# Scores of a head pair as half-row matmuls from shared tiles, and the norm's Newton turns on GpSimd

## The chip, the cores and the metric

The kernel runs on one core of a Trainium2 chip. The metric is the device time of one execution in microseconds, the median of several runs. TensorE (PE) multiplies, VectorE (DVE), ScalarE (ACT) and GpSimd (POOL) do the elementwise work, and DMAs are issued from SyncE's queue (SP).

## The reference

Two decoder layers over 1024 tokens of width 1024: a Mamba-2 layer, then a stick-breaking attention layer over 16 heads of 64 columns. Only the attention matters here. Key and query heads are RMS-normed over their 64 columns; the scores are the product over those 64 columns; the weights come from a running product along the keys.

```
k = rmsnorm(kv[..., :SB_WIDTH].reshape(bsz, s, SB_HEADS, SB_HEAD_DIM), k_g)
q = rmsnorm(qg[..., :SB_WIDTH].reshape(bsz, s, SB_HEADS, SB_HEAD_DIM), q_g)
...
z = jnp.einsum('bhtd,bhsd->bhts', q[:, :, q0:kend], k[:, :, :kend]).astype(jnp.float32)
log_keep = jnp.where(strict, jax.nn.log_sigmoid(-z), 0.0)
suffix = lax.cumsum(log_keep, axis=3, reverse=True) - log_keep
weights = jnp.where(strict, jnp.exp(jax.nn.log_sigmoid(z) + suffix), 0.0)
outs.append(jnp.einsum('bhts,bhsd->bhtd', weights.astype(v.dtype), v[:, :, :kend]))
```

## The kernel before

Every large product is made from two-part operands: a float is split into a high part (fp32r) and a low part (the rest), and three products are summed (high by high, high by low, low by high).

The attention (`attention`, from L860) goes over 8 head pairs `hp`; each pair has four steps, `p` = 3, 2, 1, 0, of 256 queries, so there are 32 steps `i`. A step projects queries, keys and values for its two blocks of 128 tokens (`project`, L923, 48 matmuls of 384 columns on L911), and at p = 1 the gate of the pair. `norm` (L1010) squares on ACT, sums on DVE (L1022), starts a reciprocal root on DVE (L1028 to L1030), improves it in three Newton turns of three small DVE instructions (L1034 to L1036, tiles of 128x8) and multiplies (`nmul`, L1043). `flip` (L1046) transposes keys and queries on PE (L1054) and splits them. In the kernel before each head has key tiles of its own in `kst`: the high part of head h in its own 64 partitions, the low part in the other 64 (L1064 on ACT, L1067 on DVE); `qh` holds the query's high part twice (L1076, four ACT copies a step), and `ql` holds the low part with zeros in the other half (L1081). So one matmul over all 128 rows gives high by high and high by low together (L1111), and a second one gives low by high (L1112).

`scores` (L1098) does that for one head h and one block of 128 queries b, in one piece up to 512 key columns or two pieces above that; then a sigmoid on ACT (L1119) and a scan on DVE (L1124). `combine` (L1130) transposes the scanned weights (L1150, L1152), splits them (L1158 ACT, L1163 DVE), and multiplies by the value differences (L1171). The value differences are formed on POOL (`values`: L997, L1006, L1007).

The order of the work is made by a planner (`Plan`, from L70): each operation is given with its engine, a cost in us, a rank, what it follows and which ring slots it takes or frees. `order()` always takes the operation that can start first by these costs, the smaller rank among equals (`RANK`, L44). The whole list is then issued in that order. For PE, ACT and DVE the list order is kept as it is (L1377); POOL and SP are not in that list, so their order is left to the framework. The score tiles `z` are a ring of two PSUM banks, the probability tiles `pt` a ring of five, `qh` of one.

Of the kernel before, what the change touches and what calls it, by code (L numbers as in the profile page):

```python
# [8 lines left out]
F32 = mybir.dt.float32  # L9
F32R = mybir.dt.float32r  # L10
# [3 lines left out]
ALU = mybir.AluOpType  # L14
# [4 lines left out]
P = 128  # L19
# [21 lines left out]
FILL = {32: 7, 33: 6}  # L41
CHUNKS = {29: (0, 1), 30: (2, 3)}

RANK = {"project": 3, "copy_kq": -13, "sums": -16, "start": -28, "newton": -2587, "nmul": -6, "v_split": -57,  # L44
        "gate": 20, "sig": 55, "gmul": -17, "w_load": 6, "w_hi": -28, "w_lo": -45, "k_hi": 10, "k_lo": -32,
        "q_hi": -853, "q_lo": -3, "scores": -1586, "s_sig": -729, "scan": 8, "turn": -2674, "a_hi": 20,
        "a_lo": 1, "o_add": -18, "o_gate": 27, "store": -4, "r_lo": -919, "o_load": 7, "o_hi": 6, "f_load": 13,
        "f_split": -10, "fill": -19, "f_add": -1544}


def split3(nc, out, pairs):
# [18 lines left out]
class Plan:  # L70
# [789 lines left out]
def attention(k, A, rawp, hT, oTd, dbg, b2, pairs):  # L860
# [6 lines left out]
    with ExitStack() as ctx:  # L867
# [13 lines left out]
        ql = pp.tile([P, 2, 256], F32R, name="ql")  # L881
        nc.gpsimd.memset(ql.bitcast(F32), 0.0)

        oqs = op.tile([P, 512], F32, name="oq")

        plan = Plan()
        for name, bufs in (("mm", 2), ("z", 2), ("tr", 3), ("w", 3), ("pt", 5), ("kq", 2), ("vr", 3), ("qh", 1), ("sg", 1),
                           ("of", 2), ("V", 6), ("vs", 1), ("raw", 3)):
            plan.ring(name, bufs)
        op_, slot = plan.op, plan.slot  # L890
# [119 lines left out]
        def norm(i, hp, p, copies):  # L1010
            g = {}
            sg_s = slot("sg")

            def square():
                g["sq"] = wk.tile([P, 512], F32, name="sg", bufs=1)
                nc.scalar.activation(g["sq"], sts[hp]["kq", p].rearrange("p b m c -> p (b m c)"), AF.Square)
            sq = op_("square", "ACT", 0.63, 10 * i + 1, square, copies, (sg_s,))
            m = 8

            def sums():  # L1020
                g["ss"] = sm.tile([P, m], F32, name="kss")
                nc.vector.reduce_sum(g["ss"], g["sq"].rearrange("p (g d) -> p g d", d=64), axis=AX.X)  # L1022
            rd = op_("sums", "DVE", 0.68, 10 * i + 1, sums, [sq], (), (sg_s,))

            def start():
                v, y = g["v"], g["y"] = [sm.tile([P, m], F32, name=x) for x in ("krv", "kry")]
                g["s"] = sm.tile([P, m], F32, name="krs")
                nc.vector.tensor_scalar(v, g["ss"], 1.0 / 64, EPS, op0=ALU.mult, op1=ALU.add)  # L1028
                nc.vector.tensor_single_scalar(y.bitcast(I32), v.bitcast(I32), 1, op=ALU.logical_shift_right)
                nc.vector.tensor_scalar(y.bitcast(I32), y.bitcast(I32), -1.0, float(0x5F3759DF), op0=ALU.mult, op1=ALU.add)  # L1030

            def turn_():
                v, y, s = g["v"], g["y"], g["s"]
# [12 lines left out]
        def flip(i, hp, p):  # L1046
# [10 lines left out]
            ks, qs = slot("tr", 2), slot("tr", 2)  # L1057
# [3 lines left out]
            qh_s = slot("qh", 2 * sum(len(parts(b)) for b in (2 * p + 1, 2 * p)))  # L1061

            def key_hi(h):
                return lambda: nc.scalar.activation(kst[own[h], h, tsl], t[0][own[h]], AF.Copy, scale=g[own[h]])  # L1064

            def key_lo(h):
                return lambda: nc.vector.scalar_tensor_tensor(  # L1067
                    kst[own[1 - h], h, tsl], t[0][own[h]], g[own[h]], kst[own[h], h, tsl].bitcast(F32),
                    op0=ALU.mult, op1=ALU.subtract)

            def query_hi(h):
                def go():
                    if h == 0:
                        tiles["qh", i] = wk.tile([P, 2, 256], F32R, name="qh", bufs=1)
                    for x in (own[h], own[1 - h]):
                        nc.scalar.copy(tiles["qh", i][x, h], t[1][own[h]])  # L1076
                return go

            def query_lo(h):
                o = own[h]  # L1080
                return lambda: nc.vector.tensor_tensor(ql[o, h], t[1][o], tiles["qh", i][o, h].bitcast(F32), op=ALU.subtract)  # L1081
            prev, pd = [], []
            for h in range(2):
                prev = [op_("k_hi", "ACT", 0.47, 10 * i + 2, key_hi(h), [fk] + prev + (old if p == 3 else []))]
                khi[i, h] = prev[0]
                pd = [op_("k_lo", "DVE", 0.49, 10 * i + 2, key_lo(h), [khi[i, h]] + pd, (), (ks,))]
                klo[i, h] = pd[0]
            for h in range(2):
                prev = [op_("q_hi", "ACT", 0.73, 10 * i + 2, query_hi(h), [fq] + prev, (qh_s,) if h == 0 else ())]
                pd = [op_("q_lo", "DVE", 0.43, 10 * i + 2, query_lo(h), prev + pd + old, (), (qs,))]  # L1090
                qlo[i, h] = pd[0]
# [6 lines left out]
        def scores(i, hp, h, b, qh_s):  # L1098
            N = (NT - b) * P
            qs = slice((b % 2) * P, (b % 2) * P + P)  # L1100
            pt_s[i, h, b] = slot("pt")
            key = ("a", hp, h, b)
            last = []
            sg = []
            for m, (ko, w) in enumerate(parts(b)):
                z_s = slot("z")

                def mul(ko=ko, w=w, m=m):
                    z = tiles["z", i, h, b, m] = zp.tile([P, 512], F32, name="z")
# [6 lines left out]
                def sig(ko=ko, w=w, m=m):  # L1116
                    if m == 0:
                        tiles[key] = wk.tile([P, S], F32, name="pt", bufs=5)
                    nc.scalar.activation(tiles[key][:, ko:ko + w], tiles["z", i, h, b, m][:, :w], AF.Sigmoid, scale=-1.0)  # L1119
                s = op_("s_sig", "ACT", 0.19 + w * 0.00078, 10 * i + 3, sig, [z] + sg, (pt_s[i, h, b],) if m == 0 else (), (z_s,))  # L1120

                def scan(ko=ko, w=w):
                    pt = tiles[key]
                    nc.vector.tensor_tensor_scan(pt[:, ko:ko + w], pt[:, ko:ko + w], keep[:, ko:ko + w],  # L1124
                                                 pt[:, ko - 1:ko] if ko else 1.0, op0=ALU.mult, op1=ALU.max)
                sg = [s]
                last = [z, op_("scan", "DVE", 0.15 + w * 0.00208, 10 * i + 3, scan, [s] + last[1:])]
            scans[i, h, b] = last[1]

        def combine(i, hp, p):  # L1130
            lo = 2 * p
# [207 lines left out]
        for hp in range(8):  # L1339
# [14 lines left out]
                begun.append(op_("begin", "SPW", 0.0, 0, lambda: b2.begin(pairs), proj[6, 0][-1:]))  # L1354
            for i, p in pair:
                qh_s = flip(i, hp, p)
                for h in range(2):
                    for b in (2 * p + 1, 2 * p):
                        scores(i, hp, h, b, qh_s)
                combine(i, hp, p)  # L1360
        for kk in range(KT):
            s_out(kk)
# [247 lines left out]
```

## Time and profile before

| what | value |
|---|---|
| median of 3 runs | 1757.9 us (1756.42 to 1758.44) |
| profiled execution | 1758.81 us |
| its span, first to last instruction | 1757.1 us |
| mean granted TensorE clock | 0.994 of full speed |
| PE busy | 1703.1 us (97%) |
| DVE busy | 1196.1 us (68%) |
| ACT busy | 895.9 us (51%) |
| POOL busy | 434.2 us (25%) |

The attention fills the stretch from about 930 to 1570 us; before it lies the Mamba layer and the first embedding, behind it the output projection and the second embedding. Instructions of PE are pipelined, so the shown duration of a matmul is longer than its share of the engine; the distance from the start of one to the start of the next is what it costs.

### The profile page before, as it was taken

The numbers are of one execution on the slowest core, as the hardware profiler recorded it, in microseconds if no ns is written. First come the engines' busy times: TensorE is split into PE (matmuls) and PEld (weight loads), VectorE is DVE, ScalarE is ACT, GpSimd is POOL, SyncE is SP. The second block draws the span as 40 slices with busy tenths as digits, with TensorE's granted clock in tenths as the row PEclk, the third lists the DMA queues.
The fourth block names the chain that finished last, engine by engine and source line by source line (L and its number), as shares of the span: only waits on it lengthen the run. The fifth ranks groups of instructions, "written<-read, shape, count | busy, mean of one in ns | idle before, by whom it ended". The sixth has DMA issues, their size and how long they took to land.

```text
span 1757.1 us, 25573 instructions
## 1 busy us (share of the span) xinstructions
PE 1703.1 (97%) x9170; PEld 1450.7 (83%) x9170; DVE 1196.1 (68%) x2460; ACT 895.9 (51%) x1976; POOL 434.2 (25%) x452
## 2 busy tenths in 40 slices
PE   7999999999999999999999999999999999899999
PEld 6777877887887777888888999989999998778887
DVE  7678179259448846443567699999999999993232
ACT  6558339447635624222355556666575666652121
POOL 0134624524444322220001111121121214211010
PEclk9999999999999999999999999999999999899999
DMA  4222213213212365332221111111110112252100
GB/s 162 69 67 91 96 49 108 90 54 96 91 66 79 126 215 179 113 132 87 82 100 31 56 32 59 41 33 56 31 59 28 48 43 67 76 165 78 57 28 36
DMA packets 96399, 139.43 MB, mean 79 GB/s; under 512 B 18160, under 2 KB 66640, under 8 KB 96272
## 3 DMA queue, kind: packets, MB, share of 16 engines
q1 hardware_dynamic: 96272, 137.80, 24.4%
q8 instruction: 72, 1.18, 0.3%
q14 instruction: 55, 0.45, 0.1%
HBM read 108.77 MB, written 24.77 MB: 76 GB/s over the span
## 4 chain that ended last, share of the span: by engine, by line
PE 79%; DVE 13%; ACT 4%; DMA 2%; issue 2%; POOL 0%; SPq 0%; DVEq 0%; ACTq 0%
PE mm L54 38%; PE mm L911 17%; PE mm L1441 4%; PE oq L1171 3%; DVE pt L1124 3%; PE pq L54 3%; DVE v L310 2%; PE intra L485 2%; PE z L1111 2%; PE z L1112 2%; PE tr L1150 1%; PE tr L740 1%; DVE wl L1163 1%; PE inter L480 1%; PE tr L1152 1%
## 5 line engine op out<-in xcount | busy, mean ns | idle before, releaser
L54 PE MATMUL mm<-ul,wh 128*128 128x512 f32 (+1 forms) x648 | 254.0, 392 | 0.0
L54 PE MATMUL mm<-uh,wh 128*128 128x512 f32 (+1 forms) x648 | 252.4, 390 | 0.1
L54 PE MATMUL mm<-uh,wl 128*128 128x512 f32 (+1 forms) x648 | 252.4, 390 | 0.0
L1124 DVE TENSOR_TENSOR_SCAN pt<-pt,keep 128x320 f32<-128x320 f32 (+3 forms) x192 | 196.1, 1048 | 3.5 <-ACT pt L1119 1.4
L911 PE MATMUL mm<-g0h,hh 128*128 128x384 f32 x512 | 174.7, 341 | 3.6 <-ACT vr L952 1.8
L911 PE MATMUL mm<-g0l,hh 128*128 128x384 f32 x512 | 175.9, 343 | 0.0
L911 PE MATMUL mm<-g0h,hl 128*128 128x384 f32 x512 | 174.2, 340 | 0.0
L310 DVE SCALAR_TENSOR_TENSOR v<-u,convh,v 128x512 f32<-128x512 f32 x144 | 129.5, 904 | 55.1 <-ACT v L308 52.6
L997 POOL TENSOR_TENSOR vs<-vs,vr 128x256 f32<-128x256 f32 x32 | 30.5, 953 | 477.4 <-DMA vs<-vr 241.1
L54 PEld LDWEIGHTS mm<-ul,wh 128*128 128x128 f32 x648 | 121.7, 188 | 26.4 <-issue 2.3
L54 PEld LDWEIGHTS mm<-uh,wl 128*128 128x128 f32 x648 | 121.8, 188 | 25.5 <-issue 1.9
L54 PEld LDWEIGHTS mm<-uh,wh 128*128 128x128 f32 x648 | 121.7, 188 | 25.5 <-issue 1.1
L182 POOL TENSOR_TENSOR wl<-raw,wh 128x1024 fp32r<-128x1024 f32 x39 | 95.1, 2440 | 156.1 <-ACT wh L180 156.0
L1158 ACT CAST wh<-tr 128x512 fp32r<-128x512 f32 (+1 forms) x160 | 84.4, 547 | 64.2 <-PE tr L1152 59.1
L650 DVE SCALAR_TENSOR_TENSOR acc<-mm,rg,acc 128x512 f32<-128x512 f32 x64 | 47.8, 749 | 84.8 <-PE mm L54 83.2
L1119 ACT ACTIVATE pt<-z 128x320 f32<-128x320 f32 (+3 forms) x192 | 87.0, 492 | 36.4 <-PE z L1112 24.3
L1163 DVE TENSOR_TENSOR wl<-tr,wh 128x512 fp32r<-128x512 f32 (+1 forms) x160 | 96.6, 629 | 7.5 <-ACT wh L1158 6.1
L911 PEld LDWEIGHTS mm<-g0h,hh 128*128 128x128 f32 x512 | 96.5, 188 | 5.8 <-DVE GT L979 2.9
L911 PEld LDWEIGHTS mm<-g0h,hl 128*128 128x128 f32 x512 | 96.6, 189 | 0.9
L911 PEld LDWEIGHTS mm<-g0l,hh 128*128 128x128 f32 x512 | 96.5, 188 | 0.6
L723 DVE SCALAR_TENSOR_TENSOR pth<-pth,pq 128x512 f32<-128x512 f32 (+1 forms) x33 | 22.2, 672 | 108.2 <-PE pq L54 103.6
L447 ACT ACTIVATE ex<-ex,acum 128x128 f32<-128x128 f32 x256 | 86.5, 389 | 0.8
(378 smaller groups left out, 4316.6 us busy)
## 6 DMA issues: line engine op xcount, KB each, us to landing
raw<-in_w_in SPq DMA_DIRECT2D x40, 512.0 KB
ex<-acd SPq DMA_DIRECT2D x64, 256.0 KB
raw<-in_w_b SPq DMA_DIRECT2D x32, 512.0 KB
raw<-in_m_out SPq DMA_DIRECT2D x16, 512.0 KB
raw<-in_gate SPq DMA_DIRECT2D x16, 512.0 KB
graw<-gT SPq DMA_DIRECT2D x30, 256.0 KB
gT<-zs SPq DMA_DIRECT2D x28, 256.0 KB
acc<-in_x SPq DMA_DIRECT2D x8, 512.0 KB
```

The source lines that it names most:

```text
L54: nc.tensor.matmul(out, lhsT=a, rhs=b, start=(i == 0), stop=(i == n - 1))
L182: (eng or nc.gpsimd).tensor_tensor(lo, raw, hi.bitcast(F32), op=ALU.subtract)
L310: nc.vector.scalar_tensor_tensor(vv, u[:, 3 - j:3 - j + 512], w(j), vv, op0=ALU.mult, op1=ALU.add)
L447: nc.scalar.activation(x, x, AF.Relu, bias=acum[:, c:c + 1])
L650: nc.vector.scalar_tensor_tensor(acc[:, sl], ps, k.rg[:, g, t:t + 1], acc[:, sl], op0=ALU.mult, op1=ALU.add)
L911: nc.tensor.matmul(out, lhsT=a, rhs=b, start=(i == 0), stop=(i == len(prs) - 1))
L1119: nc.scalar.activation(tiles[key][:, ko:ko + w], tiles["z", i, h, b, m][:, :w], AF.Sigmoid, scale=-1.0)
L1124: nc.vector.tensor_tensor_scan(pt[:, ko:ko + w], pt[:, ko:ko + w], keep[:, ko:ko + w], pt[:, ko - 1:ko] if ko else 1.0, op0=ALU.mult, op1= ...
L1158: nc.scalar.copy(wh[:, :c], tiles["tq", key][:, :c])
L1163: nc.vector.tensor_tensor(wl[:, :c], tiles["tq", key][:, :c], wh[:, :c].bitcast(F32), op=ALU.subtract)
L1171: nc.tensor.matmul(out[:, :w], lhsT=sts[hp]["V"][j // 2][:, j % 2, h * P:(h + 1) * P], rhs=rhs, start=(j0 == lo and m == 0), stop=(j0 == N ...
L1441: nc.tensor.matmul(pss[n], lhsT=a, rhs=b, start=(q == 0 and i == 0), stop=(q == 1 and i == 11))
```

## The change

- `flip` splits keys and queries once for both heads, over all 128 partitions: keys to `kst[:, 0]` (high) and `kst[:, 1]` (low), queries to `qh[:, 0]` and `qh[:, 1]`. The tile `ql` is gone, and `qh` is a ring of two.
- `scores` handles both heads of a block in one operation: for each of the three products it issues one matmul on partitions 0 to 63 (head 0) and one on partitions 64 to 127 (head 1), into two different `z` banks. An operation takes both `z` slots. The sigmoids and scans of the two heads then follow in turn.
- The three Newton turns go to POOL, each as four instructions instead of three, with a planned cost of 1.15 us a turn instead of 0.6.
- POOL joins the engines whose order is kept.
- The rank table is a new one.

```diff
-            for _ in range(3):
-                x = op_("newton", "DVE", 0.6, 10 * i + 1, turn_, [x])
+            for _ in range(3):
+                x = op_("newton", "POOL", 1.15, 10 * i + 1, turn_, [x])
...
-                nc.vector.tensor_tensor(s, y, v, op=ALU.mult)
-                nc.vector.scalar_tensor_tensor(s, s, -0.5, y, op0=ALU.mult, op1=ALU.mult)
-                nc.vector.scalar_tensor_tensor(y, s, 1.5, y, op0=ALU.add, op1=ALU.mult)
+                nc.gpsimd.tensor_tensor(s, y, v, op=ALU.mult)
+                nc.gpsimd.tensor_tensor(s, s, y, op=ALU.mult)
+                nc.gpsimd.tensor_scalar(s, s, -0.5, 1.5, op0=ALU.mult, op1=ALU.add)
+                nc.gpsimd.tensor_tensor(y, s, y, op=ALU.mult)
...
+            def key_hi():
+                nc.scalar.activation(kst[:, 0, tsl], t[0], AF.Copy, scale=g)
+            def key_lo():
+                nc.vector.scalar_tensor_tensor(
+                    kst[:, 1, tsl], t[0], g, kst[:, 0, tsl].bitcast(F32), op0=ALU.mult, op1=ALU.subtract)
+            def query_hi():
+                tiles["qh", i] = wk.tile([P, 2, 256], F32R, name="qh", bufs=2)
+                nc.scalar.copy(tiles["qh", i][:, 0], t[1])
+            def query_lo():
+                q = tiles["qh", i]
+                nc.vector.tensor_tensor(q[:, 1], t[1], q[:, 0].bitcast(F32), op=ALU.subtract)
...
-                    rk = kst[:, h, b * P + ko:b * P + ko + w]
-                    nc.tensor.matmul(z[:, :w], lhsT=tiles["qh", i][:, h, qs], rhs=rk, start=True, stop=False)
-                    nc.tensor.matmul(z[:, :w], lhsT=ql[:, h, qs], rhs=rk, start=False, stop=True)
+                    zz = [zp.tile([P, 512], F32, name="z") for _ in range(2)]
+                    for n, (x, y) in enumerate(((0, 0), (0, 1), (1, 0))):
+                        for h in range(2):
+                            tiles["z", i, h, b, m] = zz[h]
+                            o = own[h]
+                            nc.tensor.matmul(zz[h][:, :w], lhsT=q[o, x, qs], rhs=kst[o, y, ks], start=(n == 0), stop=(n == 2))
-                z = op_("scores", "PE", 2 * (0.013 + w * 0.000419), 10 * i + 3, mul, [klo[i, h], qlo[i, h]] + last[:1], (z_s,), (qh_s,))
+                z = op_("scores", "PE", 3 * (0.013 + w * 0.000419), 10 * i + 3, mul, [klo[i], qlo[i]] + last[:1],
+                        z_s, (qh_s,))
...
-        with tc.manual_schedule(engines={mybir.EngineType.PE, mybir.EngineType.Activation, mybir.EngineType.DVE}):
+        with tc.manual_schedule(engines={mybir.EngineType.PE, mybir.EngineType.Activation, mybir.EngineType.DVE, mybir.EngineType.Pool}):
```

## Rows read from the trace of the kernel before

**Rows 1.** The page's first part: busy time, share and instructions of each engine.

```profile
PE 1703.1 (97%) x9170; PEld 1450.7 (83%) x9170; DVE 1196.1 (68%) x2460; ACT 895.9 (51%) x1976; POOL 434.2 (25%) x452
```

**Rows 2.** Busy time by stretch: start:end, length, busy us (instructions) by engine, granted clock, DMA.

```profile
950.00:1475.00 525.00, 518.71 (x3200) 488.80 (x3199) 473.18 (x1045) 326.08 (x792) 99.18 (x147) 1.00 0.13 41
1475.00:1570.00 95.00, 80.98 (x448) 69.09 (x447) 88.13 (x154) 59.01 (x126) 26.12 (x22) 0.93 0.36 115
1570.00:1757.00 187.00, 183.25 (x845) 149.36 (x843) 63.26 (x171) 38.05 (x74) 17.91 (x13) 1.00 0.18 59
```

**Rows 3.** PE's waits from 930 to 1575: whom for, us, times, longest.

```profile
PE tr L1150 <- DVE wl L1163: 7.0, 6, 2.5
PE tr L1054 <- DVE kq L1043: 3.0, 1, 3.0
```

**Rows 4.** The line of the first score matmul: duration ns min/median/max, starts, forms.

```profile
L1111 PE MATMUL z<-kst,qh x192: 219/344/776, 946.4 to 1529.5; 128*128 128x384 f32 x48, 128*128 128x512 f32 x48, 128*128 128x320 f32 x32, 128*128 128x448 f32 x32
```

**Rows 5.** Timeline of PE around L341's 32-row transposes: start us, us, line, shape, count.

```profile
45.61 0.39 PE L54 MATMUL mm<-uh,wl 128*128 128x512 f32 x1
45.84 0.40 PE L54 MATMUL mm<-uh,wh 128*128 128x512 f32 x1
46.17 0.68 PE L341 MATMUL tr<-ident,BC 32*128 32x32 f32 x8
46.78 0.50 PE L54 MATMUL mm<-ul,wh 128*128 128x512 f32 x1
47.12 0.39 PE L54 MATMUL mm<-uh,wl 128*128 128x512 f32 x1
```

**Rows 6.** PE groups by line and shape: busy us, mean ns of one.

```profile
L341 PE MATMUL tr<-ident,BC 32*128 32x32 f32 x8 | 0.7, 224 | 0.0
```

**Rows 7.** Timeline of PE around L485, matmuls on halves of the columns.

```profile
410.04 0.50 PE L54 MATMUL mm<-ul,wh 128*128 128x512 f32 x1
410.47 0.66 PE L485 MATMUL intra<-ex,xdt 128*64 128x128 f32 x8
411.06 0.50 PE L54 MATMUL mm<-uh,wl 128*128 128x512 f32 x1
```

**Rows 8.** Timeline of PE around L480, matmuls on the whole array.

```profile
402.73 0.40 PE L54 MATMUL mm<-ul,wh 128*128 128x512 f32 x1
402.96 0.62 PE L480 MATMUL inter<-BC,st 128*128 128x128 f32 x4
403.34 0.47 PE L54 MATMUL mm<-uh,wl 128*128 128x512 f32 x1
403.66 0.40 PE L54 MATMUL mm<-uh,wh 128*128 128x512 f32 x1
```

**Rows 9.** The score tiles' own instructions from 950 to 1475: PE, PEld, ACT.

```profile
950.00:1475.00 525.00, 80.26 (x334) 57.40 (x334) 75.65 (x167) 1.00 0.13 41
```

**Rows 10.** DVE groups from 930 to 1570: busy us, mean ns, idle before.

```profile
L1067 DVE SCALAR_TENSOR_TENSOR kst<-tr,gkq,kst 64x256 fp32r<-64x256 f32 x64 | 30.9, 484 | 13.6 <-ACT kst L1064 12.0
...
L1081 DVE TENSOR_TENSOR ql<-tr,qh 64x256 fp32r<-64x256 f32 x64 | 26.9, 420 | 4.6 <-ACT qh L1076 2.7 <-issue 0.6
```

**Rows 11.** ACT groups from 930 to 1570.

```profile
L1076 ACT CAST qh<-tr 64x256 fp32r<-64x256 f32 x128 | 47.0, 367 | 2.5
...
L1064 ACT ACTIVATE kst<-tr,gkq 64x256 fp32r<-64x256 f32 x64 | 29.9, 468 | 6.4 <-PE tr L1054 5.9
```

**Rows 12.** Timeline of DVE: first and last of one step's nine Newton instructions.

```profile
1510.64 0.17 DVE L1034 TENSOR_TENSOR krs<-kry,krv 128x8 f32<-128x8 f32 x1
...
1512.25 0.17 DVE L1036 SCALAR_TENSOR_TENSOR kry<-krs,kry 128x8 f32<-128x8 f32 x1
```

**Rows 13.** POOL groups of the whole span: busy us, mean ns of one.

```profile
L1007 POOL TENSOR_TENSOR V<-vs,V 128x128 fp32r<-128x128 f32 x64 | 43.7, 702 | 0.0
...
L307 POOL COPY u<-u 128x3 f32<-128x3 f32 x24 | 4.9, 204 | 61.2 <-issue 41.7 <-ACT u L303 15.6 <-DVE v L310 3.9
```

**Rows 14.** Timeline of POOL in the tail: one L1007 by itself.

```profile
1518.28 0.46 POOL L1007 TENSOR_TENSOR V<-vs,V 128x128 fp32r<-128x128 f32 x1
```

More of the change, by code (lines that the diff above doesn't have):

```diff
@@ L42 @@
 CHUNKS = {29: (0, 1), 30: (2, 3)}
[L44 to L48, printed above, removed]
+RANK = {"project": -10, "copy_kq": -1654, "copy_v": -1279, "square": -1991, "sums": 1, "start": -5294,
+        "newton": -1, "nmul": 9, "v_split": -10, "gate": -2745, "sig": 3, "w_load": -52, "w_hi": -2219,
+        "w_lo": -18, "k_hi": -96, "q_hi": -1822, "scores": 8, "s_sig": -2726, "scan": 18, "a_hi": -1642,
+        "a_lo": 5, "prod": 16, "o_add": 25, "o_gate": 23, "begin": -12, "r_hi": 6, "r_lo": 40, "o_load": 42,
+        "o_hi": -1, "o_lo": 9, "f_split": 12, "fill": 23, "f_add": 29}
 def split3(nc, out, pairs):
@@ L880, in attention @@
         kst = pp.tile([P, 2, S], F32R, name="kst")
-        ql = pp.tile([P, 2, 256], F32R, name="ql")
-        nc.gpsimd.memset(ql.bitcast(F32), 0.0)
         oqs = op.tile([P, 512], F32, name="oq")
         plan = Plan()
-        for name, bufs in (("mm", 2), ("z", 2), ("tr", 3), ("w", 3), ("pt", 5), ("kq", 2), ("vr", 3), ("qh", 1), ("sg", 1),
+        for name, bufs in (("mm", 2), ("z", 2), ("tr", 3), ("w", 3), ("pt", 5), ("kq", 2), ("vr", 3), ("qh", 2), ("sg", 1),
                            ("of", 2), ("V", 6), ("vs", 1), ("raw", 3)):
@@ L1056, in flip @@
             old = list(zs.get(i - 1, ()))
-            ks, qs = slot("tr", 2), slot("tr", 2)
+            ks, qs = slot("tr"), slot("tr")
             fk = op_("flip", "PE", 0.22, 10 * i + 2, turn_(0), [nmul[i]], (ks,))
@@ L1060, in flip @@
             g = k.gkq
[L1061 to L1091, printed above, removed]
+            qh_s = slot("qh", sum(len(parts(b)) for b in (2 * p + 1, 2 * p)))
+            def key_hi():
[3 more added lines that the diff above has]
+                    kst[:, 1, tsl], t[0], g, kst[:, 0, tsl].bitcast(F32), op0=ALU.mult, op1=ALU.subtract)
@@ new lines, in query_hi @@
+            def query_hi():
[4 more added lines that the diff above has]
+                nc.vector.tensor_tensor(q[:, 1], t[1], q[:, 0].bitcast(F32), op=ALU.subtract)
+            x = op_("k_hi", "ACT", 0.45, 10 * i + 2, key_hi, [fk] + (old if p == 3 else []))
+            klo[i] = op_("k_lo", "DVE", 0.49, 10 * i + 2, key_lo, [x], (), (ks,))
@@ L1092, in flip @@
+            x = op_("q_hi", "ACT", 0.42, 10 * i + 2, query_hi, [fq], (qh_s,))
+            qlo[i] = op_("q_lo", "DVE", 0.43, 10 * i + 2, query_lo, [x], (), (qs,))
             return qh_s
@@ L1096, in parts, with scores @@
             return [(0, N)] if N <= 512 else [(0, N // 2), (N // 2, N // 2)]
-        def scores(i, hp, h, b, qh_s):
+        def scores(i, hp, b, qh_s):
             N = (NT - b) * P
             qs = slice((b % 2) * P, (b % 2) * P + P)
[L1101 to L1104, printed above, removed]
+            last, sg = [], [[], []]
+            for h in range(2):
+                pt_s[i, h, b] = slot("pt")
             for m, (ko, w) in enumerate(parts(b)):
-                z_s = slot("z")
+                z_s = [slot("z") for _ in range(2)]
@@ L1108, in mul @@
                 def mul(ko=ko, w=w, m=m):
-                    z = tiles["z", i, h, b, m] = zp.tile([P, 512], F32, name="z")
-                    rk = kst[:, h, b * P + ko:b * P + ko + w]
-                    nc.tensor.matmul(z[:, :w], lhsT=tiles["qh", i][:, h, qs], rhs=rk, start=True, stop=False)
-                    nc.tensor.matmul(z[:, :w], lhsT=ql[:, h, qs], rhs=rk, start=False, stop=True)
-                z = op_("scores", "PE", 2 * (0.013 + w * 0.000419), 10 * i + 3, mul, [klo[i, h], qlo[i, h]] + last[:1], (z_s,), (qh_s,))
@@ L1114, in scores @@
-                zs.setdefault(i, []).append(z)
[L1116 to L1125, printed above, removed]
@@ L1126, in scores @@
-                sg = [s]
-                last = [z, op_("scan", "DVE", 0.15 + w * 0.00208, 10 * i + 3, scan, [s] + last[1:])]
-            scans[i, h, b] = last[1]
+                    zz = [zp.tile([P, 512], F32, name="z") for _ in range(2)]
+                    ks = slice(b * P + ko, b * P + ko + w)
+                    q = tiles["qh", i]
+                    for n, (x, y) in enumerate(((0, 0), (0, 1), (1, 0))):
+                        for h in range(2):
+                            tiles["z", i, h, b, m] = zz[h]
+                            o = own[h]
+                            nc.tensor.matmul(zz[h][:, :w], lhsT=q[o, x, qs], rhs=kst[o, y, ks], start=(n == 0), stop=(n == 2))
@@ new lines, in scores, with sig, scan @@
+                z = op_("scores", "PE", 3 * (0.013 + w * 0.000419), 10 * i + 3, mul, [klo[i], qlo[i]] + last[:1],
+                        z_s, (qh_s,))
+                zs.setdefault(i, []).append(z)
+                sc = last[1:]
+                last = [z]
+                for h in range(2):
+                    def sig(ko=ko, w=w, m=m, h=h):
+                        if m == 0:
+                            tiles["a", hp, h, b] = wk.tile([P, S], F32, name="pt", bufs=5)
+                        nc.scalar.activation(tiles["a", hp, h, b][:, ko:ko + w], tiles["z", i, h, b, m][:, :w], AF.Sigmoid, scale=-1.0)
+                    s = op_("s_sig", "ACT", 0.19 + w * 0.00078, 10 * i + 3, sig, [z] + sg[h], (pt_s[i, h, b],) if m == 0 else (), (z_s[h],))
+                    sg[h] = [s]
+                    def scan(ko=ko, w=w, h=h):
+                        pt = tiles["a", hp, h, b]
+                        nc.vector.tensor_tensor_scan(pt[:, ko:ko + w], pt[:, ko:ko + w], keep[:, ko:ko + w],
+                                                     pt[:, ko - 1:ko] if ko else 1.0, op0=ALU.mult, op1=ALU.max)
+                    x = op_("scan", "DVE", 0.15 + w * 0.00208, 10 * i + 3, scan, [s] + sc[h:h + 1])
+                    last.append(x)
+                    scans[i, h, b] = x
@@ L1356, in attention @@
                 qh_s = flip(i, hp, p)
-                for h in range(2):
-                    for b in (2 * p + 1, 2 * p):
-                        scores(i, hp, h, b, qh_s)
+                for b in (2 * p + 1, 2 * p):
+                    scores(i, hp, b, qh_s)
                 combine(i, hp, p)
```

## The prediction

> **What bounds the kernel now.** I read the page's engine totals first: PE is busy for 97% of the span, no other engine for more than 68% [rows 1]. Such an average says nothing of a single stage, so the second view is the busy time by stretch [rows 2]. From 950 to 1475 us, the body of the attention, PE is busy for 518.7 of 525 us and DVE for 473; from 1475 to 1570, the attention's tail, PE has 14 us of idle time and DVE seven; from 1570 on nothing changes. The third view is PE's waits [rows 3]: its longest sums are on DVE (7.0 us on the split of the weights, 3.0 us once on the normed keys), little against 525 us. So in the body, time that is added to PE or taken from it goes straight into the span; work on DVE, ACT and POOL counts only where PE must wait for it; in the tail it is the other way round.
>
> **The score matmuls.** From the code: a head has N = 128, 256 ... 1024 key columns for its eight blocks, 4608 in all, so 16 heads have 73,728, and each passes through PE twice (L1111, L1112), in 192 pieces [rows 4]. Back-to-back matmuls of 512 columns start 0.23 us apart (the first two of [rows 5]), or 0.00045 us a column: 147,456 columns cost 66.4 us. Afterwards each of three products takes both heads at once, if the halves run side by side: 3 x 36,864 = 110,592 columns, 49.8 us. That saves 16.6 us. The body holds 167 of the 192 pieces [rows 9] (334 matmuls, two a piece), so 14.4 us of it count there in full.
>
> **What it costs to change how the array is divided.** The 192 pieces become 96 visits, each surrounded by matmuls and transposes on the whole array: an operation takes both z banks, so the next one must wait for two sigmoids, and PE does other work between. The trace has two places where PE leaves the whole array and returns without waiting for data. At L341 (32 rows) the start of the L54 before it and that of the second L54 behind it lie 47.12 - 45.84 = 1.28 us apart [rows 5]. Two L54 take 0.46; the eight transposes take 8 x (0.68 - 0.22) / 7 = 0.52 at their own pace [rows 5, 6]; 0.30 us are left over. At L485 (halves of the columns) the eight matmuls last 0.66 us from first start to last end where four on the whole array last 0.62 [rows 7, 8], so pairs do run side by side. But L54 to L54 with such a visit between takes 1.02 us [rows 7], and with a further L54 of 0.23 it is 1.25, where the same pattern with four whole-array matmuls takes 403.66 - 402.73 = 0.93 [rows 8]. The visit costs 0.32 us more than the work in it. What the new scores use, halves of the rows with fp32r operands, stands in no row. Of the two, L341 is the nearer (rows, not columns). The first pair of a score visit loads 128 weight columns where L485 loads 64; the L54 behind a visit, which loads 128 afresh, shows 0.50 instead of 0.40 [rows 5, 7], so up to 0.10 may come on top. I take 0.33 us a visit, ends 0.30 and 0.40.
>
> The Trainium skill, page "TensorEngine Tiling (Array Packing)", section "Key Properties", says that changing the tiling mode drains the engine and names no price; it speaks against this change, and the two visits above agree with it (0.30 and 0.32 us). Its page "TensorE: Matmul & The Clock Gate", section "Measured speedup vs the span model", prices packed matmuls at one duration plus about 4 ns for each further tile, with nothing for entering or leaving; by that the sum would end near 1739 instead of 1769, and no row here agrees with so low a price.
>
> In the body 83.5 visits x 0.33 = 27.6 us against 14.4 saved: **+13** (+10.6 to +19). The other 12.5 visits add 4.1 and save 2.2; most lie in the tail, where PE idles, so +1 (0 to 2).
>
> **The splits.** A step's two L1067 and two L1081 on 64 partitions become one each on 128, with the same columns: 64 fewer instructions of 0.45 us, 29 us less on DVE [rows 10]. Two L1064 and four L1076 become one each: 96 x 0.367 + 32 x 0.468 = 50 us less on ACT [rows 11]. Their chain ahead of a step's scores loses two of ACT's three q copies on its end and one key copy, some 1.5 us. None of it is PE's own time. PE has only 6.3 us without busy time in the body [rows 2], some of which waits for DVE; I take -3 (0 to -6).
>
> **The Newton turns.** Nine DVE instructions start 0.2 us apart, from 1510.64 to 1512.42 in the step shown [rows 12]: 1.8 us a step, 57 us in all, leave DVE. On POOL they are twelve. No POOL arithmetic on eight columns stands in the trace. The nearest row is L307's copy of three columns, 0.204 us; L1007 takes 0.46 by itself and 0.70 on average beside DVE's work, a factor of 1.5 [rows 13, 14]. So a step's turns take 12 x 0.20 = 2.4 to 12 x 0.31 = 3.7 us, and the planner's 3.45 lies between. The norm ends 0.6 to 1.9 us later, with a crossing to POOL and one back beyond that. The added wait stands on DVE: `nmul` (L1043) now waits for POOL, and behind it in DVE's kept order stand scans and weight splits, for which PE's transposes and products wait. On POOL, `v_sub` and the value splits (L997 to L1007) and in the tail the out-weight splits now queue with the turns, and L1171 waits for the values. The cover is large: in the body DVE has 52 us of idle time before the change and over 70 us less work after it, POOL is busy for 99 of 525 us [rows 2], and of PE's waits only one, in the tail, was for the normed keys [rows 3]. I take 0, ends 0 and +8 (a quarter of a microsecond in each of 32 steps). No DMA is moved; the dropped zeroing of `ql` lies ahead of the stage.
>
> **The tail.** The last norm comes about 2 us later and the splits behind it about 2 us earlier. Head 0's transposes now wait for scans of both heads, and a score operation for both banks; DVE has less to do. I take 0, ends -4 and +5.
>
> **Sum.** The profiled execution took 1758.8 us, 1.7 above its span and 0.9 above the median of the runs. 1758.8 + 13 + 1 - 3 + 0 = 1770, or 1769 against the median. Without the far ends falling together this case lies between 1760 and 1783.
>
> **The rivals.**
> - *Entering and leaving cost nothing in this form.* For it: pairs on halves of the columns do run side by side [rows 7], and the fp32r form is in no row. Against it: both visits, one of them on rows, paid 0.30 us or more. Then the body gives -14.4, the rest -1, the relief -3: 1740, or 1739 against the median. It ends on the faster side; it decides where a visit costs under 0.17 us (16.6 / 96). The span model named above is this case.
> - *The halves don't run side by side*, so the change doesn't do what it says. Six half matmuls in line are 221,184 columns, 99.5 us, +33: 1791 without the visits' price, 1823 with it. Against it are the pairs of L485 [rows 7].
> - *POOL becomes the clock of the norm.* If each small instruction waits behind a DVE instruction on its way, the turns outgrow the planned 3.45 us, and DVE stands still at `nmul` in each step. Each half microsecond that PE can't cover is 32 x 0.5 = 16 us: 1785. Against it: POOL has four fifths of the stretch free [rows 2].
>
> **How the numbers follow.** I give the forecast 0.66, the free visit 0.22, the halves in line 0.07, POOL 0.05. A measurement of this kernel can tell about 0.2%, 3.5 us, from no change. Of the forecast's 0.66, 0.06 falls within that and 0.02 below it (a cheap visit with all of the relief). So faster is 0.02 + 0.21 = 0.23, the same 0.06 + 0.01 = 0.07, slower 0.58 + 0.07 + 0.05 = 0.70. The likeliest is 1769. The range goes from 1738 to 1786: it leaves out the lower part of the free visit (0.09) and nearly all of the halves in line with some of POOL's case (0.09).
>
> **What the changed profile would show.** In the timeline of PE, a score operation is three pairs with starts a few ns apart, and from the whole-array matmul before it to the second one behind it there are 0.3 us beyond the columns' time. If that surplus is near zero, the free visit is right; if the six start one after another, the halves run in line. The attention's body should be some 10 us longer with PE as full as now, DVE's share should fall from 90% to near 75%, and PE's waits should not name the normed keys more than once or twice. The prediction is wrong if visits are fewer than about 96 because score operations stand next to one another, if their price is below 0.2 us, or if DVE's relief gives PE more than the 6 us that it visibly lacks.

## The result, and the profile after

| what | before | after |
|---|---|---|
| median | 1758.2 us (1756.4 to 1758.7) | 1807.3 us (1806.3 to 1809.4) |
| ratio, 95% interval | | 1.0283 (1.0265 to 1.0300) |
| profiled execution, its span | 1758.8, 1757.1 us | 1806.3, 1804.5 us |
| mean granted clock | 0.994 | 0.986 |

The kernel became slower by 49.1 us. The forecast had been 1769 with a range up to 1786: the sign held, the size did not. The page's engine totals (answering [rows 1]) and the windows of the attention (answering [rows 2]; start:end, length, then busy us of PE, PE's weight loads, DVE, ACT and POOL with the instructions, granted clock, DMA share, GB/s), both of the kernel after; a pair's time, further down, is the distance in PE's timeline from the end of the last projection of the third pair (hp = 2) to that of the seventh (hp = 6), divided by four:

```profile
PE 1729.4 (96%) x9362; PEld 1440.3 (80%) x9362; DVE 1113.1 (62%) x2108; ACT 847.9 (47%) x1848; POOL 516.4 (29%) x835
```

```profile
950.00:1475.00 525.00, 499.95 (x3125) 442.58 (x3124) 375.46 (x686) 265.00 (x638) 148.70 (x441) 0.98 0.13 41
1475.00:1617.00 142.00, 125.02 (x708) 104.08 (x704) 106.73 (x174) 75.77 (x161) 54.77 (x97) 0.90 0.26 83
1617.00:1804.00 187.00, 183.61 (x846) 149.71 (x846) 61.55 (x167) 36.50 (x71) 17.17 (x12) 1.00 0.17 57
```

In the same 525 us of the body PE is without work for 25 us where it had been for 6 [rows 2], and the granted clock is 0.98 where it was 1.00. The last 187 us are as before. So the time is in the attention, and a good part of it is no work of PE at all. Who PE waits for is in its waits from 930 to 1625 us (answering [rows 3]: sum, times, longest), and behind it, in DVE's and POOL's waits of the same stretch, who those wait for:

```profile
PE tr L1053 <- DVE kq L1042: 27.3, 8, 5.0
PE z L1104 <- ACT pt L1114: 4.5, 4, 3.0
...
DVE kq L1042 <- POOL kry L1035: 84.4, 29, 7.9
...
POOL vs L995 <- DMA vs<-vr: 238.5, 26, 16.4
```

The transposes of the normed keys (L1053, `flip`), which had waited 3.0 us once, now wait 27.3 us in eight waits. Behind them `nmul` (L1042) on DVE waits 84.4 us, in 29 waits over 32 steps, for the last Newton turn (L1035) on POOL. And POOL itself stands 238.5 us at `v_sub` (L995), for the DMA that shifts the values by a row.

One such step in the timelines of the kernel after (start us, us, engine, line; in brackets the idle time before and who ended it): SyncE's issue of the value DMA, DVE's last instruction of the root's start, then POOL, DVE and PE.

```profile
1144.25 0.69 SPq L986 DMA_DIRECT2D vs<-vr  x1
...
1145.21 0.17 DVE L1028 TENSOR_SCALAR kry<-kry 128x8 int32<-128x8 int32 x1
...
1153.33 0.74 POOL L995 TENSOR_TENSOR vs<-vs,vr 128x256 f32<-128x256 f32 x1 [12.46 <-DMA vs<-vr]
1154.13 0.29 POOL L1004 CAST V<-vs 128x128 fp32r<-128x128 f32 x1
...
1155.69 0.20 POOL L1032 TENSOR_TENSOR krs<-kry,krv 128x8 f32<-128x8 f32 x1
1155.97 0.20 POOL L1033 TENSOR_TENSOR krs<-krs,kry 128x8 f32<-128x8 f32 x1
...
1158.80 0.20 POOL L1035 TENSOR_TENSOR kry<-krs,kry 128x8 f32<-128x8 f32 x1
...
1159.03 0.69 DVE L1042 TENSOR_TENSOR kq<-kq,kry 128x512 f32<-128x512 f32 x1 [4.46 <-POOL kry L1035]
...
1156.11 0.34 PE L909 MATMUL mm<-g0h,hl 128*128 128x384 f32 x1
1159.78 0.66 PE L1053 MATMUL tr<-ident,kq 128*128 128x128 f32 x4 [3.33 <-DVE kq L1042]
```

The DMA is issued at 1144.25 and releases the subtraction at 1153.33, 9.1 us later (8.0 to 11.3 over the 32 steps); the planner had put it down at 3.0. In POOL's order of this step the subtraction and the value splits stand ahead of the twelve instructions of the turns, which have no need of them: DVE has started the root by 1145.38, and the turns begin 10.3 us later. So it is in 20 of the 32 steps, where the turns begin 0.7 to 11.9 us after the root's start, 115 us in all; in the other 12 they stand ahead of their own step's subtraction and begin within 0.3 us. The turns themselves go here at their planned pace: 0.28 us apart, 3.3 us from 1155.69 to the end of the last. DVE then does `nmul`, with its scans queued behind it, and PE has run out of projections 3.3 us before.

### The profile page after: what moved, and what is told of

The parts are those of the page before. It is cut to its first block, busy times and chain, and to the rows that moved or that the text cites. A ratio compares the mean times of both kernels' runs of the same rounds, so it can differ in the third digit from the quotient of the medians.

```text
span 1804.5 us, 25793 instructions
## 1 busy us (share of the span) xinstructions
PE 1729.4 (96%) x9362; PEld 1440.3 (80%) x9362; DVE 1113.1 (62%) x2108; ACT 847.9 (47%) x1848; POOL 516.4 (29%) x835
## 4 chain that ended last, share of the span: by engine, by line
PE 74%; DVE 10%; DMA 7%; POOL 3%; ACT 3%; issue 2%; SPq 0%; POOLq 0%; DVEq 0%; ACTq 0%
PE mm L54 37%; PE mm L909 15%; DMA vs<-vr 4%; PE mm L1436 4%; PE oq L1167 3%; PE pq L54 2%; PE z L1104 2%; DVE v L310 2%; PE intra L485 2%; PE tr L1146 2%; PE inter L480 1%; PE tr L1148 1%; PE tr L740 1%; DMA raw<-in_gate 1%; PE tr L464 1%
## 5 line engine op out<-in xcount | busy, mean ns | idle before, releaser
L1120 DVE TENSOR_TENSOR_SCAN pt<-pt,keep 128x384 f32<-128x384 f32 (+4 forms) x192 | 185.9, 998 | 13.0 <-ACT pt L1114 12.3
L909 PE MATMUL mm<-g0h,hh 128*128 128x384 f32 x512 | 181.2, 354 | 0.0
L909 PE MATMUL mm<-g0h,hl 128*128 128x384 f32 x512 | 178.5, 349 | 0.0
L1114 ACT ACTIVATE pt<-z 128x384 f32<-128x384 f32 (+4 forms) x192 | 85.9, 489 | 70.7 <-PE z L1104 51.5
L995 POOL TENSOR_TENSOR vs<-vs,vr 128x256 f32<-128x256 f32 x32 | 26.0, 812 | 264.5 <-DMA vs<-vr 238.5
```

The costliest lines, as they stand in the source:

```text
L909: nc.tensor.matmul(out, lhsT=a, rhs=b, start=(i == 0), stop=(i == len(prs) - 1))
L1114: nc.scalar.activation(tiles["a", hp, h, b][:, ko:ko + w], tiles["z", i, h, b, m][:, :w], AF.Sigmoid, scale=-1.0)
```

## The experiments

The theory from these profiles: the halves cost what was forecast, and the rest comes from the turns standing behind `v_sub` in POOL's queue. The rivals: small instructions on POOL are dear by themselves; the kept order of POOL is what harms; the half-row matmuls cost far more than 0.33 us a visit; the new ranks make a bad order.

### Each part alone

`scores_alone` is the kernel after with the turns back on DVE and POOL's order free:

```
-                nc.gpsimd.tensor_tensor(s, y, v, op=ALU.mult)
...
+                nc.vector.tensor_tensor(s, y, v, op=ALU.mult)
...
-                x = op_("newton", "POOL", 1.15, 10 * i + 1, turn_, [x])
+                x = op_("newton", "DVE", 0.6, 10 * i + 1, turn_, [x])
```

> The changed kernel with the Newton turns back on VectorE (three instructions, planned 0.6 us a turn) and GpSimd's order left free; the half-row scores and the new ranks stay. Theory A (96 visits at 0.35 to 0.40 us less 16.6 us of columns, the rest of the loss from turns that stand behind the value subtraction and its DMA in GpSimd's kept order): 1773 to 1783 us, and PE's waits on the normed keys nearly gone. Rival B (the scores in this form cost the whole loss, by the visits and by an operation that needs both score banks): 1797 or more. Rival C (the new ranks alone make a worse order): 1790 or more, with waits spread over other lines.

`norm_alone` is the kernel before with the turns on POOL and POOL's order kept, the same lines the other way round.

> The kernel before with only the Newton turns on GpSimd (four instructions, planned 1.15 us a turn) and GpSimd's order kept; scores and ranks as before. Theory A: slower by 15 to 35 us (1773 to 1793), with VectorE waiting some 60 us and more at the norm's multiplication. Rival B: 1754 to 1762, as VectorE only loses work.

Measured: `scores_alone` 1795.4 us, ratio 1.0212 (1.0197 to 1.0227); `norm_alone` 1794.4 us, 1.0209 (1.0194 to 1.0225). Each costs over 36 us, together they cost 49: the parts don't add up, so neither number is the price of a part. `scores_alone` missed the 1773 to 1783 us of its theory; what else it carried is taken up under the ranks. In `norm_alone` the wait is there again in DVE's waits, with 40.9 us where some 60 had been expected; its turns stand behind their own step's `v_sub` in 6 of the 32 steps:

```profile
DVE kq L1044 <- POOL kry L1037: 40.9, 12, 9.4
```

### The wait in POOL's queue

`vload9` tells the planner what the DMA takes, and nothing else:

```
-            vd[i] = op_("v_load", "SPV", 3.0, ...
+            vd[i] = op_("v_load", "SPV", 9.0, ...
```

> The changed kernel with one number changed: the planner's cost of the value load is 9.0 us, which is what its DMA takes in the trace, instead of 3.0. Theory A (the turns are late because the planner puts them behind a subtraction that waits 6 us longer for its DMA than planned): 1772 to 1788 us, VectorE's wait at the norm's multiplication down from 84 us to under 25. Rival B: 1800 to 1810, as nothing about the scores changes.

Measured: 1774.0 us, 1.0089 (1.0074 to 1.0104), 33 us less than the kernel after. Its waits, of DVE, PE and POOL:

```profile
DVE kq L1042 <- POOL kry L1035: 17.1, 16, 3.5
...
PE tr L1053 <- DVE kq L1042: 2.5, 1, 2.5
...
POOL vs L995 <- DMA vs<-vr: 27.4, 10, 6.2
```

All three links of the chain fall together: POOL's wait from 238.5 to 27.4 us, DVE's from 84.4 to 17.1, PE's from 27.3 to 2.5, and in all 32 steps the turns now stand ahead of the subtraction. But a changed cost alters the whole order, so the same edit went into three other kernels.

> Half-row scores with the Newton turns on VectorE, GpSimd's order free, and the value load planned at 9.0 us. scores_alone spent 77.2 us a head pair in the body (before: 74.1) and lost another 21 us in the tail, where ScalarE stood for 12 us at an out-weight split. Theory A: the body's loss is the visits (12 a pair at 0.42 us less 2.1 us of columns, 3.0 us a pair, 20 to 24 us over the body) and the tail's loss is the same mis-planned load, so 1777 to 1786. Rival B (the tail is made late by the scores' need of both banks): 1790 to 1798. Rival C (the new ranks): the same as B, with the tail unchanged.

> The kernel before with the Newton turns on GpSimd in a kept order, and the value load planned at 9.0 us. Theory A: the turns themselves are free and take work off VectorE; norm_alone already ran its last five pairs at 73.2 us each against 74.1. So the whole loss of norm_alone (36 us) goes: 1748 to 1760. Rival D (the turns cost by crossing to GpSimd and back): 1770 or more.

> The kernel before with only the planned cost of the value load changed, 9.0 us for 3.0: the control for the other three. In it no turn stands behind the load, so Theory A: 1752 to 1762. If it gains 10 us or more, the other runs' gains by that number are no sign of the turns' cause.

Measured: with the turns on DVE, 1795.5 us against 1795.4 (the edit does nothing, where a gain had been expected; the orders of PE, ACT, DVE and POOL come out the same, so that this run says nothing of what another order would do); the kernel before with turns on POOL, 1767.2 against 1794.4 (27 us less, though not below the kernel before as expected); the kernel before itself, 1761.5, 1.0017 (1.0008 to 1.0027). So the edit helps only where the turns are on POOL. That fits the queue; a better order of the other engines it does not rule out by itself.

`turns_first` leaves the planner's 3.0 us as they are and adds one dependency: `v_sub` follows the last turn of its own step. The planner orders the rest anew by it; 92% of PE's instructions from 900 us on keep their sequence.

```
-                x = op_("newton", "POOL", 1.15, 10 * i + 1, turn_, [x])
+                x = turned[i] = op_("newton", "POOL", 1.15, 10 * i + 1, turn_, [x])
...
-                tiles["vs", i], tiles["vs", i], sts[hp]["vr"][p], op=ALU.subtract), [vd[i]], (), (vr_s[i],))
+                tiles["vs", i], tiles["vs", i], sts[hp]["vr"][p], op=ALU.subtract), [vd[i], turned[i]], (), (vr_s[i],))
```

> The changed kernel with one dependency added in the planner: a step's value subtraction on GpSimd follows that step's last Newton turn. Costs, ranks, kept order and scores stay, and PE's list stays largely the same. Theory A (turns behind a subtraction that waits for its DMA): 1768 to 1785, VectorE's wait at the norm's multiplication under 25 us where the changed kernel has 84. Rival (vload9 gained by another order of everything, not by the turns' place): 1797 or more.

Measured: 1769.4 us, 1.0065 (1.0050 to 1.0080): 37.9 us less than the kernel after. The window of its body, and then the same kind of step in POOL's and DVE's timelines:

```profile
950.00:1475.00 525.00, 521.09 (x3313) 460.20 (x3312) 402.66 (x726) 279.32 (x672) 185.34 (x478) 1.00 0.13 41
```

```profile
1151.60 0.20 POOL L1032 TENSOR_TENSOR krs<-kry,krv 128x8 f32<-128x8 f32 x1 [3.90 <-DVE kry L1028]
...
1152.17 0.45 POOL L1034 TENSOR_SCALAR krs<-krs 128x8 f32<-128x8 f32 x1
...
1154.44 0.89 POOL L1034 TENSOR_SCALAR krs<-krs 128x8 f32<-128x8 f32 x1
...
1156.55 0.20 POOL L1035 TENSOR_TENSOR kry<-krs,kry 128x8 f32<-128x8 f32 x1
1157.68 0.92 POOL L995 TENSOR_TENSOR vs<-vs,vr 128x256 f32<-128x256 f32 x1 [0.93 <-ACT pt L1114]
...
1157.32 0.68 DVE L1042 TENSOR_TENSOR kq<-kq,kry 128x512 f32<-128x512 f32 x1
```

POOL now waits ahead of the turns for DVE's start of the root, not for a DMA, and `nmul` starts 0.57 us after the last turn's end, with no idle time of DVE before it. PE is busy for 521.1 of 525 us and the clock is back at 1.00. The turns take longer here (5.2 us from 1151.60 to 1156.75, single ones up to 0.89) than in the kernel after (3.3), and it doesn't matter: that speaks against POOL's own speed as the cause.

The page's engine totals of this run and its waits of PE, DVE and POOL tell where the gain lies:

```profile
PE 1719.8 (97%) x9362; PEld 1430.1 (81%) x9362; DVE 1112.3 (63%) x2108; ACT 847.2 (48%) x1848; POOL 541.3 (31%) x835
```

```profile
PE tr L1053 <- DVE kq L1042: 0.3, 1, 0.3
...
DVE kq L1042 <- POOL kry L1035: 16.7, 15, 3.5
...
POOL vs L995 <- DMA vs<-vr: 41.0, 15, 6.2
```

The profiled span falls by 37.3 us, from 1804.5 to 1767.2. PE is without work for 27.7 us less (75.1 to 47.4), and its wait for the normed keys, 27.3 to 0.3, makes 27.0 of them. The other 9.6 us are busy time of PE for the same 9362 instructions (1729.4 to 1719.8), at a mean granted clock of 0.986 in the kernel after and 0.993 here. So next to nothing is left that a better order of the rest could have brought.

`pool_free` is the kernel after with POOL's order left to the framework (`mybir.EngineType.Pool` taken out of the kept engines).

> The changed kernel with GpSimd's order left to the framework again, turns on GpSimd, planned cost 3.0. The framework's list puts nearly every step's turns behind that step's value subtraction, the steps included in which the kept order has them ahead. Theory A (what hurts is the place behind the load, whoever chose it): no better than the changed kernel, 1803 to 1830. If keeping the order is itself what hurts: 1770 to 1790.

Measured: 1811.3 us, 1.0298 (1.0284 to 1.0312). DVE still waits 73.5 us in 29 waits for the turns and PE 26.9 us for `nmul`. The framework's order has the turns behind their own step's `v_sub` in 19 of the 32 steps, where nearly all had been expected, so it is much the same order. Keeping it is not the fault: with the order free, the turns wait all the same.

### The price of a score visit

`whole_array` makes the scores from three matmuls on all 128 rows with the same columns and the same planned cost, so that the array's division isn't changed. It leaves out the separation of the heads: each matmul sums over the rows of both, so its scores are not those of the reference:

```
-                    for n, (x, y) in enumerate(((0, 0), (0, 1), (1, 0))):
-                        for h in range(2):
-                            tiles["z", i, h, b, m] = zz[h]
-                            o = own[h]
-                            nc.tensor.matmul(zz[h][:, :w], lhsT=q[o, x, qs], rhs=kst[o, y, ks], start=(n == 0), stop=(n == 2))
+                    for h, x, y, n in ((1, 0, 0, 2), (0, 0, 0, 0), (0, 0, 1, 1)):
+                        tiles["z", i, h, b, m] = zz[h]
+                        nc.tensor.matmul(zz[h][:, :w], lhsT=q[:, x, qs], rhs=kst[:, y, ks], start=(n != 1), stop=(n != 0))
```

> The changed kernel in its own order with the six half-row matmuls of a score operation replaced by three whole-array matmuls of the same width (head 1 gets one product, head 0 two, and each contracts over both heads' rows, so the scores are not the reference's). The columns that PE streams are the same; only the leaving and entering of the whole array is gone. Theory A: 96 x 0.35 to 0.40 us less, 1768 to 1776. Visits free: 1805 to 1809. Rival B with all the loss in the visits: 1755 to 1760.

> The changed kernel with the value load planned at 9.0 us and the six half-row matmuls of a score operation replaced by three whole-array matmuls of the same width (head 1 gets one product, head 0 two, over both heads' rows, so the scores are not the reference's): the run without visits to be set against vload9 (1774.0), in an order in which PE hardly waits. Theory A: 96 visits at 0.35 to 0.42 us less, 1734 to 1742. If the visits are cheap (0.17 us): 1758.

Measured: `whole_array` 1792.8 us, 14.5 less than the kernel after (0.15 us a visit); on top of `vload9`, 1751.1, 23.0 less than `vload9` (0.24 a visit). Both gains are below the 31 us and more that had been expected. The first is small because PE is without work for 42 of the body's 525 us there, and 25 in the kernel after: what a visit saves goes into the wait. In the second, the pairs in the middle take 75.8 and 72.0 us, 0.32 for each of a pair's 12 visits; why less arrives at the end was not settled. PE's timelines of `vload9` and of `whole_vload9`, each around a score operation between two projections:

```profile
1125.23 0.33 PE L909 MATMUL mm<-g0h,hl 128*128 128x384 f32 x1
1125.49 0.96 PE L1104 MATMUL z<-kst,qh 64*128 64x512 f32 x6
1126.38 0.44 PE L909 MATMUL mm<-g0h,hh 128*128 128x384 f32 x1
1126.66 0.34 PE L909 MATMUL mm<-g0l,hh 128*128 128x384 f32 x1
```

```profile
1141.81 0.34 PE L909 MATMUL mm<-g0h,hh 128*128 128x384 f32 x1
1141.99 0.78 PE L1102 MATMUL z<-kst,qh 128*128 128x448 f32 x3
1142.60 0.34 PE L909 MATMUL mm<-g0l,hh 128*128 128x384 f32 x1
1142.78 0.34 PE L909 MATMUL mm<-g0h,hl 128*128 128x384 f32 x1
```

A projection matmul starts 0.17 us after the one ahead. With half rows, from the start of the last projection ahead to that of the second behind there are 1.43 us; two projections take 0.35 and three passes of 512 columns 0.69, so 0.39 are left over (0.40 is the median of the 45 places of this kind in that trace). On the whole array it is 0.97, less 0.35 and 0.60 for three times 448 columns: 0.02. Three passes cost three passes in both, so the halves do run side by side, and the surplus is that of changing the division of the array.

`scores_oldrank` is `scores_alone` with the rank table of the kernel before; `oldrank_whole` is the same with the three matmuls of `whole_array`.

> scores_alone (half-row scores, turns on VectorE, GpSimd free) with the old rank table in place of the new one. scores_alone lost about 21 us more than before in the tail, in a place where ScalarE stood behind one out-weight split for 12 us; the load's planned cost did not change its order, so that part of the theory fell. If the tail's loss comes from the order that the new ranks give to this graph: 1775 to 1785. If it comes from the scores' form (both banks, both heads' scans ahead of the first transpose): 1790 to 1798 again.

> scores_oldrank (1781.1 us) with three whole-array matmuls of the same width in place of the six half-row ones (head 1 gets one product, head 0 two, over both heads' rows, so the scores are not the reference's). The price of leaving and entering the whole array without any turn on GpSimd. At the 0.32 us a visit that vload9 and whole_vload9 give per head pair: 1781 less 25 to 31, 1750 to 1756. If the loss of scores_oldrank came from both banks being needed by one operation: 1772 or more.

Measured: 1781.1 us, 1.0131 (1.0117 to 1.0145), and 1750.3, 0.9950 (0.9932 to 0.9969). Here PE is nearly full in the body (520.2 and 514.4 of 525 us), and the difference is 30.8 us, 0.32 us for each of the 96 visits; in the middle, at 75.7 and 72.2 us a pair, it is 0.29. The price that was forecast was 0.33.

### The ranks

`newrank` is the kernel before with only the new rank table.

> The kernel before with only the new rank table. If the new ranks are a cause of their own: slower by 10 us or more, 1768 to 1795. If they only suit the new graph: within 10 us of before, 1752 to 1768.

Measured: 1792.9 us, 1.0194 (1.0180 to 1.0208). The new table costs the old kernel 35 us, and with the halves it costs 14.3 (1795.4 against 1781.1, turns on DVE). Its longest sums among PE's waits are

```profile
PE mm L911 <- DVE GT L979: 10.6, 4, 8.9
PE z L1111 <- ACT qh L1076: 6.4, 4, 2.7
```

No single wait makes up the 35 us; why the table does so badly there stays open. It shows why `scores_alone` carried more than its part: the table makes a poor order of those operations too. `norm_alone` has the old table; of its 36.5 us, 27 go with the planned cost of the load. In `scores_alone` one place where the order costs time can be read in ACT's timeline:

```profile
1538.94 0.55 ACT L1113 ACTIVATE pt<-z 128x448 f32<-128x448 f32 x1
1551.89 1.04 ACT L1269 CAST hh<-raw 128x1024 fp32r<-128x1024 f32 x1 [12.40 <-DMA raw<-in_s_out]
```

In the attention's tail ACT stands 12.4 us at a load of the output projection; SyncE's issue of a load from there had waited up to 14.8 us for a split on POOL (L1259 for L1276), which in turn waits its turn behind `v_sub`.

### Turns on POOL without the halves

`mixed` is the kernel before with the turns on POOL in the pairs hp = 1 to 5 only, POOL's order kept and `v_load` at 9.0.

> The kernel before with the Newton turns on GpSimd for head pairs 1 to 5 alone (VectorE for 0, 6 and 7), order kept, value load planned at 9.0 us. norm_vload9 ran its middle at 73.1 us a pair against 74.1 and lost that again in the first step after the start and in the tail. If those two places are all that it lost: 1750 to 1756, faster than before. If not: 1757 to 1768.

Measured: 1757.7 us, 0.9998 (0.9989 to 1.0007): no gain. A pair takes 72.8 us in the middle, against 74.1 before, so the relief of DVE is real there, some 6 us over five pairs, and it is lost again at the ends. Where at the ends was not settled.

## Why the prediction was right in sign and wrong in size

The measured medians set the steps in a row:

| step | median us | difference |
|---|---|---|
| before | 1758.2 | |
| halves, whole array instead (`oldrank_whole`) | 1750.3 | -7.9 |
| halves as they are (`scores_oldrank`) | 1781.1 | +30.8 |
| with the new ranks (`scores_alone`) | 1795.4 | +14.3 |
| turns on POOL, ahead of `v_sub` (`turns_first`) | 1769.4 | -26.0 |
| turns behind `v_sub`, as in the change | 1807.3 | +37.9 |

The ranks' 14.3 and the turns' -26.0 are not prices of their own: the new ranks without the turns on POOL make a poor order, and the next step, in which POOL's order is kept too, more than takes it back.

- **The columns** (forecast -16.6, and a relief of -3): the columns are supported in size, the relief does not show. The pair in the middle falls from 74.1 to 72.2 us in `oldrank_whole`, 1.9 a pair or 15 us in eight. Of that only 7.9 us arrive at the end; the other 7 are lost outside the middle pairs, by what was not settled.
- **The visits** (forecast 0.33 us each, 0.30 to 0.40): right. 0.32 from the pair of kernels whose PE is nearly full, 0.29 and 0.32 from the pairs in the middle, 0.39 in the single place shown; why a place between two projections pays more than the mean was not settled. The rows of L341 and L485 [rows 5, 7] were a sound price for a form that stood in no row. The rival of a free visit falls, and so do the halves in line (0.02 us over for the same three passes on the whole array). The Trainium skill, "TensorEngine Tiling (Array Packing)", section "Key Properties", says that changing the mode drains the engine. The 0.32 us agree with that, though no run shows that the drain is what they pay for. Each visit saves 36,864 / 96 = 384 columns, 0.17 us, and pays 0.32.
- **The Newton turns** (forecast 0, ends 0 and +8): this is the step that failed. It named POOL's queue, saying that `v_sub` and the value splits "now queue with the turns", and it asked who waits behind the turns. It did not ask what the turns wait behind. (Their own length, put at 2.4 to 3.7 us a step, was 3.3 in the step of the kernel after and 5.2 in that of `turns_first`; that is not what was paid for.) In POOL's kept order `v_sub` stands ahead of them in 20 of the 32 steps, and `v_sub` waits for a DMA. It also took POOL's free time (99 of 525 us busy, [rows 2]) for cover: much of that time was POOL standing at this very instruction, and what is queued behind it can't use it. The trace before had it, in POOL's waits of the same stretch, which the forecast didn't read:

```profile
POOL vs L997 <- DMA vs<-vr: 241.1, 18, 26.6
```

  241 us before, 238.5 after: the wait is not new. New is that the norm, for which PE's transposes wait, stands behind it. Its price is the 37.9 us between `turns_first` and the change; in the profiles, 27.7 us more of PE without work and 9.6 of slower work.
- **The rival "POOL as clock of the norm"** (1785, chance 0.05) had the right place, DVE standing still at `nmul` in each step, and the wrong reason: not slow instructions, which `turns_first` shows to be harmless even at 5.2 us a step, but the queue. It was also too small: it took half a microsecond a step that PE can't cover, and the queue cost 37.9 / 32 = 1.2.
- **The tail** (forecast 0, -4 to +5): without the queue it holds. A pair in the middle of `turns_first` takes 75.8 us, 1.7 more than before. From the end of the projections of hp = 6 to the end of the span it takes 332.0 us, before 329.7: 2.3 more, of which 1.7 are the last pair's, so the tail adds about 0.6. The first three pairs together are 1.0 us longer, not 5; that is why `turns_first` is 11.2 us longer in all and not 14.
- **What the changed profile was to show**: three pairs of halves side by side, with 0.39 us over, seen. About 96 visits: 94, as two of them hold two score operations. A body some 10 us longer: 1.7 us a pair in `turns_first`, but 6.9 in the kernel after (81.0 against 74.1). DVE's share near 75%: 375 of 525, 72%. PE as full as before: no, 95% against 99%. PE's waits on the normed keys "not more than once or twice": eight times. That last sign marked the step that was wrong.

With the queue put right, the change takes 1769.4 us, which is what the forecast gave for it. The forecast had worked out a kernel whose POOL queue doesn't block, and for the pairs in the middle its sum holds: a pair's 12 visits at 0.33 us less 2.1 of columns are 1.9 us, and 1.7 were measured. That the total agrees to a microsecond is luck: the same halves with the turns on DVE take 1781.1 us with the old ranks and 1795.4 with the new, and the forecast had put nothing down for the order.

## What to carry to other kernels

Before work moves to another engine, read that engine's waits, not only its idle time: where its queue stands at a DMA, whatever is put behind that instruction inherits the wait, and a planner that takes the DMA for a third of its true time will put it there. Leaving and re-entering the whole array has a price of about 0.32 us here, some 700 columns; packed matmuls pay only where one visit saves more than that. A part of a change tested alone, in an order that came with the whole, measures the order as much as the part: change the one dependency that the theory names (here one entry in a list), and see from the waits whether it accounts for the gain, since the rest of the order moves with it.

## What the runs showed of the hardware

- A 128x8 instruction on POOL takes 0.20 us by itself and starts 0.28 after the one ahead. In the step of `turns_first` above, with DVE at work, single ones took up to 0.89 us, others 0.20; that DVE is the reason is not shown. The same turns as nine DVE instructions had started 0.2 us apart [rows 12].
- The first whole-array matmul behind a visit lasts 0.44 us where the next lasts 0.34, and it takes 0.28 instead of 0.17 until the next one starts (1126.38 to 1126.66): part of the visit's price is paid behind it. Its weight load starts together with it, where the one behind whole-array scores starts 0.20 us ahead of its matmul (1142.40 for 1142.60). The two loads, of `vload9` and of `whole_vload9`:

```profile
1126.38 0.19 PEld L909 LDWEIGHTS mm<-g0h,hh 128*128 128x128 f32 x1 [0.36 <-issue]
```

```profile
1142.40 0.19 PEld L909 LDWEIGHTS mm<-g0l,hh 128*128 128x128 f32 x1
```

- The granted clock averaged 0.98 in the body of the kernel after, where PE had 25 us without work in it, and was at its full level of 2.4 GHz (1.00) in `turns_first`, where it had 4. Over the whole span the means are 0.986 and 0.993, and PE is busy for 9.6 us more in the first for the same instructions: about a quarter of what the queue cost. That PE's waits brought the clock down is not shown apart from that.
